# Dense experts of a PEER block: output blocks of three key rows instead of two, u split in halves

## The chip, the cores and the metric

The kernel runs on one core of a Trainium2 chip. The metric is the device time of one execution in microseconds (us), as the median of three runs. A profile of one further execution shows the engines: PE (TensorE, matmuls), PEld (its weight loads), DVE (VectorE), ACT (ScalarE), POOL (GpSimd) and SP, which issues DMA transfers.

## The reference, cut to what matters

One encoder layer over 1024 tokens of width 1024: a gated mixer of attention and convolution, then `h + PEER(RMSNorm(h))`, then a final RMSNorm. The change lies in PEER. It has 128 x 128 experts; each token picks 128 of them (8 heads, 16 each), with a gate each:

```
u = expert_u[eidx]
a = gelu(einsum('chkd,cd->chk', u, xc))
vv = expert_v[eidx]
return einsum('chk,chkd->cd', g * a, vv)
```

## The kernel before

The 8 token tiles of 128 are worked in two groups. The first five (`NB`) take the **dense** path: for each of the 128 key rows `i` (`NK`), all 128 experts of that row are computed for all 640 tokens, and the gate (`w_d`, zero where a token did not choose the expert) masks them. The last three (`NA`) take the **gather** path: for each token tile and each of its 128 choices, an indirect DMA on POOL brings one u row and one v row per token (`uvt`, L739, 128 x 2048 floats), DVE makes the dot product (L749), ACT the gelu and the gate (L751, L752), DVE adds the gated v row to `acc` (L754). That makes 3 x 128 = 384 such steps, called experts here, over four buffers of `uvt`. Both paths run side by side after the scores are done, from about 1316 us of the span to its end.

A key row `i` of the dense path is this chain. `expert_in(i)` loads u (`raw`, three buffers that u and v share), splits it into a high part (cast on ACT, L896) and a low part (subtract on DVE, L898), does 48 matmuls of 320 columns into `z` (L905; high x high, high x low, low x high), gelu on ACT (L929), multiplies by the gate tile `wt` on DVE (L930) and splits the product `p` in the same way. `expert_v(i)` loads and splits v. `expert_out` does p times v for ten output tiles of 128 x 512. Four of them (`held`) stay in PSUM until the end; six (`pout`, two PSUM buffers) are added to `hacc` in SBUF on DVE (L957) after each block of `BLK` key rows.

The order within an engine is set in three steps: the code's order; `tick`, which deals out the gather steps and the selection of experts by a running sum of matmul time (`GATHER`, 1.9 us a step); and a scheduler at build time, which may move an instruction past others of its engine and then fixes each engine's queue. On the chip each queue runs in that order. At the end `finish_rows` adds the held tiles, normalizes the five dense tiles and writes them out, while the rest of the gather steps runs.

Of the kernel before, what the change touches and what calls it, by code (L numbers as in the profile page):

```python
# [10 lines left out]
F32 = mybir.dt.float32  # L11
BF16 = mybir.dt.bfloat16
F32R = mybir.dt.float32r
I32 = mybir.dt.int32
U32 = mybir.dt.uint32
AF = mybir.ActivationFunctionType
# [4 lines left out]
P = 128  # L21
S = 1024
D = 1024
NT = S // P
KD = D // P
NB = 5
NA = NT - NB
GB = NB * P
# [7 lines left out]
NK = 128  # L36
# [6 lines left out]
NE = PH * TOPK  # L43

UVT = 4
PHB = 4
VHB = 3
BLK = 2
NR = 2
WB = 4  # L50
WT = 32
WQ = 4
WFB = 2
# [12 lines left out]
def block_kernel(ctx, tc, x, wqkv, wcols, wpr, wo, wq, skT, uv, uT, an_w, fn_w, fin_w, sub_w,  # L66
                 conv_w, lq1, lk1, lq2, lk2, cosT, sinT, out):
    nc = tc.nc
    V, A, PL, PE, SP = nc.vector, nc.scalar, nc.gpsimd, nc.tensor, nc.sync
# [4 lines left out]
    def pool(name, bufs=1, stack=None, **kw):  # L74
        return (stack or left).enter_context(tc.tile_pool(name=name, bufs=bufs, **kw))
# [19 lines left out]
    w_d = dram.tile([GB // WT, P, NK, WT], F32, name="w_d")  # L95
# [10 lines left out]
    def rows_bcast(pl, src, n, name, tag=None, bufs=None):  # L106
        t = pl.tile([P, n], F32, name=name, tag=tag or name, bufs=bufs)
        SP.dma_start(out=t, in_=bass.AP(tensor=src.tensor, offset=src.offset, ap=[[0, P], [1, n]]))
        return t
# [38 lines left out]
    def tick(us):  # L148
        for g in list(gens):
            g[1] -= us  # L150
            while g in gens and g[1] <= 0:
                g[1] += g[2]
                r = next(g[0], "end")
                if r == "end":
                    gens.remove(g)
                elif r:
                    g[2] = r
# [7 lines left out]
    def rstd_of(ss, n, width, tag):  # L165
        m = tiny.tile([P, width], F32, name=f"m_{tag}", tag=f"m_{tag}")
        V.tensor_scalar(m, ss, 1.0 / n, EPS, op0=ALU.mult, op1=ALU.add)
        r = tiny.tile([P, width], F32, name=f"r_{tag}", tag=f"r_{tag}")
        PL.tensor_tensor(r, m, mhalf[:, :width], op=ALU.pow)
        return r  # L170
# [9 lines left out]
    def operand(pl, shape, name, tag=None):  # L180
        return tuple(pl.tile(shape, F32R, name=name + c, tag=(tag or name) + c) for c in "hl")
# [276 lines left out]
    def halves(n):  # L458
        return [(0, n)] if n <= 512 else [(0, n // 2), (n // 2, n // 2)]
# [398 lines left out]
    n = NA * P  # L858
# [11 lines left out]
    hh, hl = operand(act, [P, KD, GB + 2], "actT")  # L870
# [17 lines left out]
    du, dn, dv, hp, gat = (pool(n) for n in ("du", "dn", "dv", "hp", "gat"))  # L888
# [1 line left out]
    hacc = hp.tile([P, NB - NR, D], F32, name="hacc")  # L890
    held = [[ps_r.tile([P, 512], F32, name=f"held{t}{hf}") for hf in range(2)] for t in range(NR)]

    def split(t, tag, bufs, shape, eng):
        pl = du if tag == "uh" else dv
        hi = pl.tile(shape, F32R, name=tag, tag=tag, bufs=bufs)
        A.copy(out=hi, in_=t)  # L896
        lo = pl.tile(shape, F32R, name=f"{tag}l", tag=f"{tag}l", bufs=bufs)
        eng.tensor_sub(lo, t, hi.bitcast(F32))  # L898
        return hi, lo

    def passes(ps, lhs, rhs, cols, first=True, last=True):
        n = len(lhs)
        for k in range(n):
            for j, (a, b) in enumerate(((0, 0), (0, 1), (1, 0))):
                PE.matmul(ps, lhsT=lhs[k][a], rhs=rhs[k][b],  # L905
                          start=first and k == 0 and j == 0, stop=last and k == n - 1 and j == 2)
        tick(cols / 2400 * 3 * n)

    wts = {}

    def raw_rows(src):
        t = du.tile([P, D], F32, name="raw", tag="raw", bufs=3)
        SP.dma_start(out=t, in_=src)
        return t

    def expert_in(i):
        b = i // WB
        if i % WB == 0:
            wts[b] = dn.tile([P, GB // WT, WB, WT], F32, name="wt", tag="wt", bufs=2)
            SP.dma_start(out=wts[b], in_=w_d[:, :, i:i + WB, :].rearrange("c p i t -> p c i t"))  # L920
        ur = raw_rows(uT[i])
        u = split(ur, "uh", 2, [P, D], V)
        us = [(u[0][:, k * P:(k + 1) * P], u[1][:, k * P:(k + 1) * P]) for k in range(KD)]
        hs = halves(GB)
        z = ps_z.tile([P, 2, 512], F32, name="z", tag="z")[:, :len(hs), :hs[0][1]]
        for j, (c0, cn) in enumerate(hs):
            passes(z[:, j, :], us, [(hh[:, k, c0:c0 + cn], hl[:, k, c0:c0 + cn]) for k in range(KD)], cn)
        p = dn.tile([P, GB], F32, name="pr", tag="pr", bufs=1)
        A.activation(p.rearrange("p (h c) -> p h c", h=len(hs)), z, AF.Gelu)  # L929
        V.tensor_mul(p.rearrange("p (c t) -> p c t", t=WT), p.rearrange("p (c t) -> p c t", t=WT),  # L930
                     wts[b][:, :, i % WB, :])
        return split(p, "ph", PHB, [P, GB], V)

    def expert_v(i):
        vr = raw_rows(uv[i * P:(i + 1) * P, D:])
        return split(vr, "vh", VHB, [P, D], V)

    resident = [(t, hf) for t in range(NR) for hf in range(2)]
    moving = [(t, hf) for t in range(NR, NB) for hf in range(2)]
    order = []  # L940
# [3 lines left out]
                order.append(q.pop(0))  # L944

    def expert_out(pv, vv, part, first, last):
        n = len(order) // BLK
        for t, hf in order[part * n:(part + 1) * n]:
            ds = slice(hf * 512, (hf + 1) * 512)
            lhs = [(p[0][:, t * P:(t + 1) * P], p[1][:, t * P:(t + 1) * P]) for p in pv]  # L950
            rhs = [(v[0][:, ds], v[1][:, ds]) for v in vv]
            if t < NR:
                passes(held[t][hf], lhs, rhs, 512, first, last)
            else:
                ps = ps_v.tile([P, 512], F32, name="pout", tag="v")
                passes(ps, lhs, rhs, 512)
                V.tensor_add(hacc[:, t - NR, ds], ps, hacc[:, t - NR, ds])  # L957

    def finish_rows():
        fin_b = rows_bcast(du, fin_w, D, "fin_d", "raw", 3)  # L960
        ss = tiny.tile([P, NB], F32, name="ss_f", tag="ss_f", bufs=1)
        ys = []
        for t in range(NB):
            if t < NR:
                y = raw_rows(h_d[t * P:(t + 1) * P, :])
                for hf in range(2):
                    ds = slice(hf * 512, (hf + 1) * 512)
                    V.tensor_add(y[:, ds], held[t][hf], y[:, ds])
            else:
                y = hacc[:, t - NR, :]  # L970
            A.activation(du.tile([P, D], F32R, name="uh", tag="uh", bufs=2), y, AF.Square, accum_out=ss[:, t:t + 1])
            ys.append(y)
        yield
        r = rstd_of(ss, D, NB, "f")
        yield
        for t in range(NB):
            V.scalar_tensor_tensor(ys[t], ys[t], r[:, t:t + 1], fin_b, op0=ALU.mult, op1=ALU.mult)
            SP.dma_start(out=out[t * P:(t + 1) * P, :], in_=ys[t])
            yield

    pv, vv = [], []
    for i in range(NK + BLK):
        if i < NK:
            pv.append(expert_in(i))
        b, part = i // BLK - 1, i % BLK
        if b >= 0:
            expert_out(pv[:BLK], vv[:BLK], part, b == 0, b == NK // BLK - 1)
            if part == BLK - 1:
                pv, vv = pv[BLK:], vv[BLK:]
        if i < NK:  # L990
            vv.append(expert_v(i))
        if i == 1:
            for t in range(NR, NB):
                SP.dma_start(out=hacc[:, t - NR, :], in_=h_d[t * P:(t + 1) * P, :])
    drain(sel)
    if gather in gens:
        gens.remove(gather)
    rows = finish_rows()
    for n in (6, 6, 1, 1, 1):
        next(rows)  # L1000
# [59 lines left out]
```

## Time and profile before

| what | value |
|---|---|
| median of 3 runs | 3186.92 us (3186.16 to 3197.02) |
| the profiled execution | 3202.99 us, span of its instructions 3201.2 us |
| PE busy | 3023.5 us (94%) |
| DVE busy | 2648.8 us (83%) |
| ACT, POOL busy | 1300.8 us (41%), 928.5 us (29%) |

The rows further down are from the trace of that profiled execution. Times are us from the start of its span. A row of the view by windows begins with the stretch and its length; then, where all engines are shown, follow the busy us and the number of instructions (x) of PE, PEld, DVE, ACT and POOL, then the mean granted PE clock (1.00 is full speed), the busy share of the 16 DMA engines and GB/s. A timeline row is start, duration, engine, line and operation; in square brackets stand the idle time ahead of it and what ended that.

### The profile page before, as it was taken

What the parts mean: (1) busy time and instruction counts of PE and PEld (TensorE: products, weight loads), DVE (VectorE), ACT (ScalarE), POOL (GpSimd) and SP (SyncE); (2) the same over time, 40 slices, a digit from 0 to 9 for tenths busy, and PEclk for the clock granted to TensorE, in tenths of its full rate; (3) what the DMA queues carried; (4) which work ended last, traced back from release to release, by engine and by line L of the source; (5) the groups of instructions that cost most, each with busy time, mean ns of one, the idle gap of its engine ahead of it and who ended that gap; (6) DMA issues with size and microseconds to landing.
All of it is one profiled execution on the core that took longest, in us unless ns stands there. A gap on an engine that the chain in (4) does not pass through costs nothing.

```text
span 3201.2 us, 45898 instructions
## 1 busy us (share of the span) xinstructions
PE 3023.5 (94%) x17551; PEld 2773.3 (87%) x17551; DVE 2648.8 (83%) x4661; ACT 1300.8 (41%) x2341; POOL 928.5 (29%) x712
## 2 busy tenths in 40 slices
PE   7999999898989989799999999999999999999994
PEld 6799998798988879789989989899898999999993
DVE  5442466379999996799999999999988999999998
ACT  3322364336567766433333333333333333333332
POOL 2310000036344444222332322222222323332333
PEclk9999999999999989899999999999999999999997
DMA  4451232555444375769888888798888999998987
GB/s 179 145 181 66 83 113 79 199 172 212 145 171 168 135 282 190 255 246 329 311 282 328 316 292 307 278 329 314 302 318 319 345 342 335 341 347 321 340 318 276
DMA packets 237549, 801.11 MB, mean 250 GB/s; under 512 B 18832, under 2 KB 123280, under 8 KB 174096
## 3 DMA queue, kind: packets, MB, share of 16 engines
q0 software_dynamic: 64704, 442.53, 37.3%
q1 hardware_dynamic: 152592, 305.30, 27.6%
q10 hardware_dynamic: 20032, 50.34, 4.1%
q8 instruction: 138, 2.26, 0.3%
q14 instruction: 83, 0.68, 0.1%
HBM read 714.74 MB, written 83.36 MB: 249 GB/s over the span
## 4 chain that ended last, share of the span: by engine, by line
PE 40%; issue 21%; DVE 16%; POOL 9%; DMA 9%; ACT 4%; SPq 0%; POOLq 0%; ACTq 0%; DVEq 0%
PE z L905 9%; POOL uvt L739 8%; PE pout L905 5%; PE pg L228 4%; PE held L905 4%; PE pq L228 3%; DMA uvt<-in_uv,idx 3%; PE ph L228 3%; DVE acc L754 2%; PE py L228 2%; DVE uvt L749 2%; PE pw L695 1%; PE ps L376 1%; PE pv L228 1%; DVE ms L714 1%
## 5 line engine op out<-in xcount | busy, mean ns | idle before, releaser
L739 POOL DMA_INDIRECT uvt<-in_uv,idx x384 | 533.2, 1389 | 1288.1 <-DVE acc L754 937.3
L905 PE MATMUL z<-actTh,uhl 128*128 128x320 f32 x2048 | 638.0, 312 | 4.0 <-DVE uhl L898 4.0
L905 PE MATMUL z<-actTh,uh 128*128 128x320 f32 x2048 | 637.4, 311 | 4.0 <-ACT pr L929 3.0
L905 PE MATMUL z<-actTl,uh 128*128 128x320 f32 x2048 | 637.0, 311 | 0.0
L749 DVE SCALAR_TENSOR_TENSOR uvt<-uvt,hng 128x1024 f32<-128x1024 f32 x384 | 471.4, 1230 | 54.3 <-DMA uvt<-in_uv,idx 53.6
L754 DVE SCALAR_TENSOR_TENSOR acc<-uvt,wt,acc 128x1024 f32<-128x1024 f32 x384 | 495.0, 1289 | 1.6 <-ACT wt L752 1.2
L905 PEld LDWEIGHTS z<-actTh,uh 128*128 128x128 f32 x2048 | 387.7, 189 | 15.7 <-ACT pr L929 3.7
L905 PEld LDWEIGHTS z<-actTh,uhl 128*128 128x128 f32 x2048 | 388.3, 190 | 11.6 <-DVE uhl L898 5.6
L905 PEld LDWEIGHTS z<-actTl,uh 128*128 128x128 f32 x2048 | 387.8, 189 | 9.9
L905 PE MATMUL pout<-vh,ph 128*128 128x512 f32 x768 | 304.0, 396 | 26.9 <-DVE hacc L957 14.0
L905 PE MATMUL pout<-vhl,ph 128*128 128x512 f32 x768 | 302.6, 394 | 0.6 <-DVE vhl L898 0.6
L905 PE MATMUL pout<-vh,phl 128*128 128x512 f32 x768 | 301.8, 393 | 0.0
L957 DVE TENSOR_TENSOR hacc<-pout,hacc 128x512 f32<-128x512 f32 x384 | 260.1, 682 | 21.2 <-PE pout L905 20.5
L718 POOL TENSOR_TENSOR o<-ms,wtr 128x512 f32<-128x512 bf16 x160 | 203.5, 1314 | 254.8 <-PE pw L695 134.8
L185 DVE TENSOR_TENSOR wl<-wr,wh 128x2048 fp32r<-128x2048 f32 x66 | 157.8, 2392 | 113.0 <-ACT wh L184 112.8
L751 ACT ACTIVATE wt<-zt 128x1 f32<-128x1 f32 x384 | 77.0, 201 | 417.0 <-DVE uvt L749 410.8
L896 ACT CAST uh<-raw 128x1024 fp32r<-128x1024 f32 x128 | 134.3, 1049 | 211.3 <-DMA raw<-in_uT 204.5
L184 ACT CAST wh<-wr 128x2048 fp32r<-128x2048 f32 x74 | 141.1, 1908 | 168.0 <-DMA wr<-in_wq 44.7
L695 PE MATMUL pw<-o,o 128*128 128x128 f32 x1280 | 172.3, 288 | 36.9 <-POOL o L718 19.4
L695 PEld LDWEIGHTS pw<-o,o 128*128 128x128 f32 x1280 | 164.4, 202 | 44.7 <-POOL o L718 25.3
L929 ACT ACTIVATE pr<-z 128x640 f32<-128x640 f32 x128 | 90.1, 704 | 275.4 <-PE z L905 254.6
L905 PE MATMUL held<-vhl,ph 128*128 128x512 f32 x512 | 200.3, 392 | 0.1
(290 smaller groups left out, 6758.6 us busy)
## 6 DMA issues: line engine op xcount, KB each, us to landing
raw<-in_uT SPq DMA_DIRECT2D x128, 512.0 KB
raw<-in_uv SPq DMA_DIRECT2D x128, 512.0 KB
w_d<-wbuf ACTq DMA_DIRECT2D x20, 2048.0 KB
wt<-w_d SPq DMA_DIRECT2D x32, 1280.0 KB
wr<-in_wcols SPq DMA_DIRECT2D x28, 1024.0 KB
wr<-in_wq SPq DMA_DIRECT2D x24, 1024.0 KB
xt<-in_x SPq DMA_DIRECT2D x16, 512.0 KB
q_d<-qt POOLq DMA_DIRECT2D x32, 256.0 KB
```

The lines of the kernel that those rows point to most:

```text
L184: A.copy(out=op[0][sl], in_=src)
L185: lo.tensor_sub(op[1][sl], src, op[0][sl].bitcast(F32))
L228: PE.matmul(pd, lhsT=l[a], rhs=r[b], start=i == 0 and j == 0, stop=i == n - 1 and j == len(c) - 1)
L695: PE.matmul(pw[:, u, :], lhsT=o2[:, t + u, :], rhs=o1[:, t + u, :], start=True, stop=True)
L718: PL.tensor_tensor(out=o1.rearrange("p t i -> p i t"), in0=ms[:, 0], in1=w[:, ts].unsqueeze(1).broadcast_to(sh), op=ALU.mult)
L739: PL.indirect_dma_start(out=t[:], out_offset=None, in_=uv, in_offset=bass.IndirectOffsetOnAxis(ap=sels[c][1][:, k:k + 1], axis=0))
L749: V.scalar_tensor_tensor(u, u, 1.0, st[c], op0=ALU.mult, op1=ALU.mult, accum_out=zt)
L754: V.scalar_tensor_tensor(st["acc"], v, wt, st["acc"], op0=ALU.mult, op1=ALU.add)
L896: A.copy(out=hi, in_=t)
L905: PE.matmul(ps, lhsT=lhs[k][a], rhs=rhs[k][b], start=first and k == 0 and j == 0, stop=last and k == n - 1 and j == 2)
L929: A.activation(p.rearrange("p (h c) -> p h c", h=len(hs)), z, AF.Gelu)
L957: V.tensor_add(hacc[:, t - NR, ds], ps, hacc[:, t - NR, ds])
```

## The change

Output blocks grow from two key rows to three (`BLK`), so `pout` and `held` gather nine matmuls instead of six before a tile is done, and 128 rows make 43 blocks, the last of two rows. u is cast and subtracted in two halves of 512 columns, each with its own buffers (three instead of two of the full width), and the matmuls of `z` take the first half for both column halves of `z`, then the second. The gate tile holds three key rows instead of four; p gets five buffers (was four), v gets four (was three).

```diff
-PHB = 4
-VHB = 3
-BLK = 2
+PHB = 5
+VHB = 4
+BLK = 3
-WB = 4
+WB = 3
...
     def expert_in(i):
-        b = i // WB
+        b, n = i // WB, min(WB, NK - i // WB * WB)
         if i % WB == 0:
             wts[b] = dn.tile([P, GB // WT, WB, WT], F32, name="wt", tag="wt", bufs=2)
-            SP.dma_start(out=wts[b], in_=w_d[:, :, i:i + WB, :].rearrange("c p i t -> p c i t"))
+            SP.dma_start(out=wts[b][:, :, :n, :], in_=w_d[:, :, i:i + n, :].rearrange("c p i t -> p c i t"))
         ur = raw_rows(uT[i])
-        u = split(ur, "uh", 2, [P, D], V)
-        us = [(u[0][:, k * P:(k + 1) * P], u[1][:, k * P:(k + 1) * P]) for k in range(KD)]
         hs = halves(GB)
         z = ps_z.tile([P, 2, 512], F32, name="z", tag="z")[:, :len(hs), :hs[0][1]]
-        for j, (c0, cn) in enumerate(hs):
-            passes(z[:, j, :], us, [(hh[:, k, c0:c0 + cn], hl[:, k, c0:c0 + cn]) for k in range(KD)], cn)
+        kh = KD // 2
+        for h in range(2):
+            u = split(ur[:, h * 512:(h + 1) * 512], "uh", 3, [P, 512], du)
+            us = [(u[0][:, k * P:(k + 1) * P], u[1][:, k * P:(k + 1) * P]) for k in range(kh)]
+            for j, (c0, cn) in enumerate(hs):
+                xs = [(hh[:, k, c0:c0 + cn], hl[:, k, c0:c0 + cn]) for k in range(h * kh, h * kh + kh)]
+                passes(z[:, j, :], us, xs, cn, h == 0, h == 1)
...
     def expert_out(pv, vv, part, first, last):
-        n = len(order) // BLK
-        for t, hf in order[part * n:(part + 1) * n]:
+        cut = [-(-len(order) * j // BLK) for j in range(BLK + 1)]
+        for t, hf in order[cut[part]:cut[part + 1]]:
...
-    for i in range(NK + BLK):
+    blocks = -(-NK // BLK)
+    for i in range((blocks + 1) * BLK):
...
-            expert_out(pv[:BLK], vv[:BLK], part, b == 0, b == NK // BLK - 1)
+            expert_out(pv[:BLK], vv[:BLK], part, b == 0, b == blocks - 1)
```

In the changed file the cast is L895, the subtract L897, the matmul L904, gelu L931, the gate L932 and the add to `hacc` L958.

On PE, in the middle of the dense path (near key row 90), the queue of before finishes a `pout` tile with two rows' p and v, three matmuls for each:

```order
L905 MATMUL pout_24515<-vh_24168,ph_24111 128x512
L905 MATMUL pout_24515<-vhl_24170,ph_24111 128x512
L905 MATMUL pout_24515<-vh_24168,phl_24113 128x512
L905 MATMUL pout_24515<-vh_24297,ph_24239 128x512
L905 MATMUL pout_24515<-vhl_24299,ph_24239 128x512
L905 MATMUL pout_24515<-vh_24297,phl_24241 128x512
```

The changed queue does so with three rows' (the same place):

```order
L904 MATMUL pout_24698<-vh_24057,ph_23995 128x512
L904 MATMUL pout_24698<-vhl_24059,ph_23995 128x512
L904 MATMUL pout_24698<-vh_24057,phl_23997 128x512
L904 MATMUL pout_24698<-vh_24184,ph_24138 128x512
L904 MATMUL pout_24698<-vhl_24186,ph_24138 128x512
L904 MATMUL pout_24698<-vh_24184,phl_24140 128x512
L904 MATMUL pout_24698<-vh_24318,ph_24265 128x512
L904 MATMUL pout_24698<-vhl_24320,ph_24265 128x512
L904 MATMUL pout_24698<-vh_24318,phl_24267 128x512
```

So the matmuls are as many as before (48 + 30 for each key row), and the tiles that DVE adds to `hacc` go from 3 to 2 for each key row, 384 to 258 in all.

On ACT, at the same place in the changed program, the casts of v for rows of the next block (`vh_24584` takes the buffer of `vh_24057`, which the matmuls just shown read last) stand ahead of the gather's gates and of the next gelu:

```order
L895 CAST ph_24666<-pr_24663 128x640
L895 CAST vh_24584<-raw_24582 128x1024
L895 CAST vh_24718<-raw_24716 128x1024
L751 ACTIVATE wt_22799<-zt_22797 128x1
L752 ACTIVATE wt_22799<-wt_22799,gw_12971 128x1
L895 CAST vh_24857<-raw_24855 128x1024
L751 ACTIVATE wt_22827<-zt_22825 128x1
L931 ACTIVATE pr_24792<-z_24726 128x640
```

Three casts of v stand together here, of which the first two wait for the last `pout` of the block before; in the queue of before it is two casts at a time.

On DVE, at the end of the program, the queue of before runs like this from its last adds to `hacc` on (L749 and L754 are the two halves of a gather step, L977 the final rows):

```order
L957 TENSOR_TENSOR hacc<-pout,hacc 128x512 x2
L754 SCALAR_TENSOR_TENSOR acc<-uvt,wt,acc 128x1024
L749 SCALAR_TENSOR_TENSOR uvt,zt<-uvt,hng 128x1024
L167 TENSOR_SCALAR m_f<-ss_f 128x5
L754 SCALAR_TENSOR_TENSOR acc<-uvt,wt,acc 128x1024
L749 SCALAR_TENSOR_TENSOR uvt,zt<-uvt,hng 128x1024
L754 SCALAR_TENSOR_TENSOR acc<-uvt,wt,acc 128x1024
L977 SCALAR_TENSOR_TENSOR raw<-raw,r_f,fin_d 128x1024 x2
L977 SCALAR_TENSOR_TENSOR hacc<-hacc,r_f,fin_d 128x1024 x3
L754 SCALAR_TENSOR_TENSOR acc<-uvt,wt,acc 128x1024
L749 SCALAR_TENSOR_TENSOR uvt,zt<-uvt,hng 128x1024 x3
L754 SCALAR_TENSOR_TENSOR acc<-uvt,wt,acc 128x1024 x3
```

The changed queue runs like this from its last add to `hacc` on:

```order
L958 TENSOR_TENSOR hacc<-pout,hacc 128x512
L749 SCALAR_TENSOR_TENSOR uvt,zt<-uvt,hng 128x1024
L754 SCALAR_TENSOR_TENSOR acc<-uvt,wt,acc 128x1024
L167 TENSOR_SCALAR m_f<-ss_f 128x5
L749 SCALAR_TENSOR_TENSOR uvt,zt<-uvt,hng 128x1024
L754 SCALAR_TENSOR_TENSOR acc<-uvt,wt,acc 128x1024
L749 SCALAR_TENSOR_TENSOR uvt,zt<-uvt,hng 128x1024
L978 SCALAR_TENSOR_TENSOR raw<-raw,r_f,fin_d 128x1024 x2
L978 SCALAR_TENSOR_TENSOR hacc<-hacc,r_f,fin_d 128x1024
L754 SCALAR_TENSOR_TENSOR acc<-uvt,wt,acc 128x1024
L978 SCALAR_TENSOR_TENSOR hacc<-hacc,r_f,fin_d 128x1024 x2
L749 SCALAR_TENSOR_TENSOR uvt,zt<-uvt,hng 128x1024 x2
```

Behind the rows shown, and up to the last L754, 23 L754 and 20 L749 stand in the changed queue. Behind its last add to `hacc` an L749 is followed at once by its own L754 in 13 places of the changed queue, and in 2 of that of before. The gather steps have moved back against the dense ones: ahead of the multiply by the gate of the 64th key row stand 170 of the 384 L754 in the queue of before and 168 in the changed one, ahead of the last such multiply 369 and 350; behind the last add to `hacc` stand 9 L754 and 7 L749 before, 26 and 25 in the changed queue.

## Rows read from the trace of the kernel before

**Rows 1.** View by windows, all engines, dense path and end.

```profile
1316.50:1348.90 32.40, 16.97 (x98) 16.36 (x99) 14.91 (x49) 8.88 (x9) 4.97 (x4) 0.81 1.02 373
1348.90:1787.60 438.70, 434.73 (x2400) 394.14 (x2400) 425.98 (x745) 147.28 (x299) 124.24 (x88) 0.99 0.84 299
...
2478.40:3133.50 655.10, 655.10 (x3666) 598.44 (x3666) 611.75 (x774) 228.13 (x484) 211.75 (x148) 1.00 0.92 336
3133.50:3159.90 26.40, 20.98 (x80) 14.86 (x78) 25.79 (x37) 10.36 (x25) 9.06 (x7) 0.94 0.83 301
3159.90:3201.20 41.30, 0.00 (x0) 0.00 (x0) 27.14 (x32) 5.78 (x18) 12.25 (x8) 0.53 0.68 247
```

**Rows 2.** View by windows, L930 alone (DVE, one for each key row).

```profile
1348.90:1787.60 438.70, 25.22 (x31) 0.99 0.84 299
1787.60:2244.30 456.70, 26.11 (x32) 1.00 0.85 306
2244.30:2478.40 234.10, 13.05 (x16) 0.99 0.86 312
2478.40:3133.50 655.10, 38.61 (x47) 1.00 0.92 336
```

**Rows 3.** Waits from 1360 to 2480 us: total, times, longest.

```profile
ACT vh L896 <- PE pout L905: 95.4, 30, 9.7
...
PE pout L905 <- DVE hacc L957: 11.4, 7, 4.8
```

**Rows 4.** Timeline of DVE from 3155 us to the end.

```profile
3158.71 1.28 DVE L957 TENSOR_TENSOR hacc<-pout,hacc 128x512 f32<-128x512 f32 x2
3159.91 1.27 DVE L754 SCALAR_TENSOR_TENSOR acc<-uvt,wt,acc 128x1024 f32<-128x1024 f32 x1
...
3166.89 2.48 DVE L977 SCALAR_TENSOR_TENSOR raw<-raw,r_f,fin_d 128x1024 f32<-128x1024 f32 x2
...
3172.87 1.28 DVE L754 SCALAR_TENSOR_TENSOR acc<-uvt,wt,acc 128x1024 f32<-128x1024 f32 x1
3174.07 1.22 DVE L749 SCALAR_TENSOR_TENSOR uvt<-uvt,hng 128x1024 f32<-128x1024 f32 x1
3175.21 0.08 DVE L749 DVE_READ_ACCUMULATOR uvt<-uvt,hng 128x1 f32 x1
...
3191.00 1.22 DVE L749 SCALAR_TENSOR_TENSOR uvt<-uvt,hng 128x1024 f32<-128x1024 f32 x1 [2.70 <-DMA uvt<-in_uv,idx]
...
3192.83 1.28 DVE L754 SCALAR_TENSOR_TENSOR acc<-uvt,wt,acc 128x1024 f32<-128x1024 f32 x1 [0.60 <-ACT wt L752]
...
3196.17 1.28 DVE L769 SCALAR_TENSOR_TENSOR acc<-acc,r_o,uvt 128x1024 f32<-128x1024 f32 x1 [0.68 <-POOL r_o L169]
```

**Rows 5.** View by windows, L754 alone (DVE, one for each expert).

```profile
2478.40:3133.50 655.10, 188.63 (x148) 1.00 0.92 336
...
3159.90:3201.20 41.30, 11.53 (x9) 0.53 0.68 247
```

**Rows 6.** Groups by line: subtract of u; busy, mean ns, idle before.

```profile
L898 DVE TENSOR_TENSOR uhl<-raw,uh 128x1024 fp32r<-128x1024 f32 x128 | 157.3, 1229 | 20.5 <-ACT uh L896 20.5
```

**Rows 7.** The chain that ended last, at the start of the dense path.

```profile
1326.33 20.00 DMA wt<-w_d
```

**Rows 8.** DMA view, 2400 to 3000 us: packets, MB, share of 16 engines; issues.

```profile
q0 software_dynamic: 19175, 139.66, 62.0%
q1 hardware_dynamic: 41152, 61.09, 29.7%
...
wt<-w_d SPq DMA_DIRECT2D x11, 1280.0 KB
```

**Rows 9.** Waits of DVE from 3159.9 us to the end.

```profile
DVE uvt L749 <- DMA uvt<-in_uv,idx: 7.0, 4, 2.7
```

**Rows 10.** Timeline of POOL near the end.

```profile
3182.76 1.95 POOL L739 DMA_INDIRECT uvt<-in_uv,idx  x1 [6.65 <-DVE acc L754]
```

More of the change, by code (lines that the diff above doesn't have):

```diff
@@ L891, in block_kernel, with split @@
     held = [[ps_r.tile([P, 512], F32, name=f"held{t}{hf}") for hf in range(2)] for t in range(NR)]
-    def split(t, tag, bufs, shape, eng):
-        pl = du if tag == "uh" else dv
+    def split(t, tag, bufs, shape, pl):
         hi = pl.tile(shape, F32R, name=tag, tag=tag, bufs=bufs)
@@ L897, in split @@
         lo = pl.tile(shape, F32R, name=f"{tag}l", tag=f"{tag}l", bufs=bufs)
-        eng.tensor_sub(lo, t, hi.bitcast(F32))
+        V.tensor_sub(lo, t, hi.bitcast(F32))
         return hi, lo
@@ L931, in expert_in @@
                      wts[b][:, :, i % WB, :])
-        return split(p, "ph", PHB, [P, GB], V)
+        return split(p, "ph", PHB, [P, GB], dv)
     def expert_v(i):
-        vr = raw_rows(uv[i * P:(i + 1) * P, D:])
-        return split(vr, "vh", VHB, [P, D], V)
+        return split(raw_rows(uv[i * P:(i + 1) * P, D:]), "vh", VHB, [P, D], dv)
     resident = [(t, hf) for t in range(NR) for hf in range(2)]
@@ L970, in finish_rows @@
                 y = hacc[:, t - NR, :]
-            A.activation(du.tile([P, D], F32R, name="uh", tag="uh", bufs=2), y, AF.Square, accum_out=ss[:, t:t + 1])
+            A.activation(dv.tile([P, D], F32R, name="vh", tag="vh", bufs=VHB), y, AF.Square, accum_out=ss[:, t:t + 1])
             ys.append(y)
```

## The prediction

> **What bounds the kernel now.** I read the view by windows first, over the stretch in which dense and gather path run side by side. From 2478.4 to 3133.5 us PE is busy in every microsecond of 655.1 [rows 1], and the gate multiply, one for each key row, comes 47 times in it [rows 2]: 655.1 / 47 = 13.94 us is what a key row costs PE with nothing in its way. That is the floor. The change keeps all 78 matmuls of a key row, so it keeps the floor.
>
> The other stretches are then held against it [rows 2]: 31 rows in 438.7 us are 6.6 us over it, 32 in 456.7 are 10.6 over, 16 in 234.1 are 11.1 over, 28 us in all. In these DVE is nearly full (425.98 of 438.7 us [rows 1]), and the waits name it: PE waited 11.4 us for adds to `hacc` [rows 3]. At the start of the dense path PE stands 15.4 of 32.4 us, and after the last gate multiply 5.4 of 26.4 [rows 1].
>
> Last, the end. After 3159.9 us PE does nothing for 41.3 us [rows 1]; DVE works there on the final rows [rows 4] and on the nine L754 that are left [rows 5], and the last of these ends the kernel. So there are two limits in a row: PE to about 3158 us, then whatever gather work DVE's queue still holds behind the dense work. The change acts on both.
>
> **The change part by part.** All durations on DVE below are spacings, from the start of one instruction to that of the next, since the rows' own durations overlap a little: an add to `hacc` 0.60 us (two in 1.20), L754 1.20, L749 1.14, the five final multiplies 5.98 together; an L749 followed at once by its own L754 costs 1.83 - 1.14 = 0.69 more, in which ACT makes the gate [rows 4].
>
> *Adds to `hacc`.* 126 of 384 go: 126 x 0.60 = 76 us, 0.59 us for each key row. *u in halves.* The subtract of 1024 columns takes 1.229 us [rows 6]; a half lies between half of it and the 0.68 us or so of an add of the same width, so two halves cost 0 to 0.13 us more. I take 0.1. ACT casts one piece more for each row and stands more than half of the time (147.28 busy of 438.7 us [rows 1]): nothing. So DVE gets back 0.5 us of each row. What that is worth is only the 28 us that PE loses in the middle, since after 2478 us PE loses nothing that could come back. Bounds 0 and 28; the first rows' DVE is also laden with the selection of experts, so I take 18. At the start PE waits for the first gate tile, which lands 20.0 us after its issue [rows 7]. It gets a quarter smaller, but the second one is now queued on SP right behind it. Between 5 us gained (a quarter of 20.0) and as much lost; I take 0.
>
> *Gate tiles of three rows.* A load still has 20 x 128 = 2560 runs, now of 384 bytes, and there are 43 loads instead of 32. Price of one load: the gathers' queue q0 moves 139.66 MB in 0.62 x 600 us, 375 KB/us; queue q1 used 0.297 x 600 = 178 us for 61.09 MB, of which 11 gate tiles are 14.4 MB [rows 8]. If the other 46.7 MB went at q0's rate (124 us), a gate tile took 54 / 11 = 4.9 us of all 16 engines. A changed load lies between 3.7 (by bytes) and 4.9 (by packets). At 4.9 the 43 take 54 us more than the 32, 0.4 us for each row. Against it stand fewer gathers in each row (next part): 148 L754 in 47 rows are 3.15 a row [rows 2, 5], the changed queue has 182 in the last 64 rows, 2.84; at 1.05 MB each that is 0.9 us less. The engines' share of 0.92 [rows 1] does not rise: nothing. But no row shows runs of 384 bytes, and a price of twice 4.9 us is not excluded: 43 x 9.8 - 32 x 4.9 = 265 us, 2.1 for each row, and the engines would be wanted for 0.92 x 13.94 + 2.1 - 0.9 = 14.0 us, just over PE's 13.94. (A rule speaks against this part too: the Trainium skill, "DMA: Bandwidth & Descriptors", section Specifications, asks for transfers of at least 512 bytes for full rate, and says that the engine reads, modifies and writes below that; by it the sum would be the one of the third rival below, by the rows it is the one I take.)
>
> *Five buffers of p and four of v, for blocks of three.* The cast of v that takes the buffer of the block before waits for the last `pout` of that block, and ACT's queue behind it holds gates of gathers and the next gelu. Such waits exist already (30 of them, 95.4 us, at most 9.7 [rows 3]), and PE loses little by them. In the changed queue that `pout` stands ahead of a whole run of 48 z matmuls (about 7 us), and two casts and two subtracts behind it need some 4.5 us before PE asks for them. I take 0; the price if the cover fails is among the rivals.
>
> *The place of the gathers.* This decides. DVE takes its queue in order, and the changed queue has 350 of 384 L754 ahead of the last gate multiply instead of 369. DVE has room for more there, but can't use it, because the steps stand further back. So first, from the last gate multiply to the last add to `hacc`: 8 L749, 8 L754, 10 adds, 4 adds of held tiles (0.60 each) and 2.6 us of splits and gate make 8 x 1.14 + 8 x 1.20 + 14 x 0.60 + 2.6 = 29.7 us, where before took 26.4 [rows 1]: +3. Then, behind the last add: 25 L749, 26 L754, the final multiplies and 13 places with the gate in the open: 28.5 + 31.2 + 6.0 + 9.0 = 74.7 us. The same sum for before (7, 9, 6.0, two places) gives 26.2; it took from 3159.9 to 3194.0, 34.1, and 7.0 of the difference are waits for gathers to land [rows 4, 9]. The changed tail thus takes between 74.7 (no wait) and 100 (one us for each gather, as now). A gather issued into an almost empty DMA took from 3182.76 to 3191.00 to be there [rows 4, 10], 8.2 us; with 3.0 for its L749 and L754 a buffer turns in 11.3 us, and four buffers give one each 2.8 us, under the 3.0 of the places with the gate in the open, a little over the 2.34 of the others. So few waits: 84. That is 50 more than before (41 to 66).
>
> **Sum.** -18 + 0 + 3 + 50 = +35 us on the profiled 3203 us, 1.1%. The profiled execution lies 0.5% over the median of the runs, so I carry the ratio over: 3187 x 3238 / 3203 = 3222 us. With all bounds for it -28 - 5 + 2 + 41 = +10 (3197), with all against it +5 + 5 + 66 = +76 (3263).
>
> **The rivals.** *PE gets all its idle time back.* If the room on DVE also cures the start and the last outputs, 28 + 15.4 + 5.4 = 49 us return, and against the 53 us of the longer tail that leaves +4: about 3191, not slower. For it: most of PE's named waits are on DVE. Against it: the start waits for a transfer, and the last outputs for DVE, which has more there than before. It decides from 37 us returned on (then less than 16 us, 0.5%, are left, about what a measurement of this kernel can tell from no change). Chance 0.14, of it 0.03 for a result faster than that.
>
> *The gathers don't go faster when they are alone.* Now one comes each 655.1 / 148 = 4.43 us [rows 5]. At that pace 25 take 111 us and the final multiplies 6: 33 more than I take, 3255. Against it: that pace is set by DVE's queue, busy 611.75 of 655.1 us [rows 1]. Chance 0.10.
>
> *The short runs fill the DMA engines*, as worked out above: u then lands late, and PE waits from the end of the selection on. For 64 rows at 0.1 to 0.5 us that is +6 to +32 on the forecast, about 3240. No row speaks for a doubled price but none excludes it. Chance 0.06.
>
> *The buffers are one short.* If of a wait of 9.7 us [rows 3] the 7 us of the z run cover only that much, 2.7 us in each of 43 blocks are 116 us: 3338, or half of it. Against it stands the order of the queues. Chance 0.05.
>
> **How the numbers follow.** My forecast, a longer tail with PE somewhat less hindered, has 0.65, with 3203 to 3245 as its own range; 0.05 of it may fall within 0.5%. Faster by over 0.5%: 0.03. Within 0.5%: 0.09 of the first rival and 0.05 of the forecast, 0.14. Slower by over 0.5%: the rest, 0.83. The range from 3194 to 3256 leaves out about half of the first two rivals and all of the last: 0.2 or a little less.
>
> **What would show it.** In the profile after: 2 adds to `hacc` for each row; in the middle, key rows at 13.9 to 14.0 us once the selection is over, with DVE at 80 to 88% instead of 93 and its waits on PE and on gathers larger; the last gate multiply some 18 us earlier (0 to 30); PE ending about 15 us earlier; and then about 90 us instead of 41 in which only DVE, POOL and ACT work, at 2.9 to 3.3 us for each gather. I am wrong if the tail is that long but PE ends 40 us or more earlier (first rival), if rows stay over 14.3 us with DVE waiting (buffers, or u landing late), or if the gathers of the tail come at over 4 us.

## The result and the profile after

The changed kernel is slower: 3233.82 us median (3230.21 to 3235.95, 4 runs) against 3190.36 us of before (3186.16 to 3197.02, 4 runs), a ratio of 1.0133 with a 95% interval of 1.0110 to 1.0156. Its profiled execution took 3230.21 us, with a span of 3228.4. In it the first gate multiply stands at 1341.0 us, the last at 3103.9, and the last add to `hacc` is over at 3133.7. The view by windows, cut there, answers to [rows 1]; columns as there.

```profile
1316.50:1341.00 24.50, 10.71 (x71) 10.19 (x69) 12.10 (x51) 6.37 (x8) 4.00 (x4) 0.82 1.03 396
1341.00:1787.60 446.60, 440.66 (x2452) 401.52 (x2453) 433.36 (x842) 158.94 (x339) 147.63 (x90) 0.99 0.84 300
...
2478.40:3103.90 625.50, 625.50 (x3506) 572.17 (x3505) 532.06 (x697) 212.16 (x479) 184.16 (x129) 1.00 0.87 314
3103.90:3133.70 29.80, 21.86 (x85) 16.01 (x83) 29.77 (x41) 10.62 (x28) 9.14 (x8) 0.94 0.77 270
3133.70:3228.40 94.70, 0.00 (x0) 0.00 (x0) 69.79 (x85) 14.74 (x54) 35.84 (x25) 0.50 0.83 303
```

DVE is relieved (532 of 625.5 us late in the dense path, 85%, where it was 93%), PE hardly stands any more, and then come 94.7 us without PE, where before had 41.3. The same view for the gate multiply alone (now L932), which answers to [rows 2]:

```profile
1787.60:2230.00 442.40, 27.82 (x32) 1.00 0.85 312
2230.00:2478.40 248.40, 14.77 (x18) 1.00 0.88 315
2478.40:3103.90 625.50, 36.11 (x44) 1.00 0.87 314
```

94 rows in 1316.3 us are 14.00 us a row; from the first gate multiply to the last, 127 rows in 1762.9 us, it is 13.88. So the floor of 13.94 is reached. The waits from 1360 to 2480 us, as [rows 3] (total, times, longest):

```profile
DVE hacc L958 <- PE pout L904: 25.6, 24, 2.0
ACT vh L895 <- PE pout L904: 20.4, 14, 3.0
...
PE pout L904 <- DVE hacc L958: 2.6, 2, 2.4
```

Now DVE waits for PE's outputs, and PE's wait for `hacc` fell from 11.4 us (7.3 in a second profile of before, e1 below) to 2.6. The timeline of DVE in the tail, as [rows 4]:

```profile
3133.05 0.68 DVE L958 TENSOR_TENSOR hacc<-pout,hacc 128x512 f32<-128x512 f32 x1
3133.82 1.23 DVE L749 SCALAR_TENSOR_TENSOR uvt<-uvt,hng 128x1024 f32<-128x1024 f32 x1
...
3163.91 1.22 DVE L749 SCALAR_TENSOR_TENSOR uvt<-uvt,hng 128x1024 f32<-128x1024 f32 x1
...
3165.74 1.28 DVE L754 SCALAR_TENSOR_TENSOR acc<-uvt,wt,acc 128x1024 f32<-128x1024 f32 x1 [0.60 <-ACT wt L752]
3166.94 1.22 DVE L749 SCALAR_TENSOR_TENSOR uvt<-uvt,hng 128x1024 f32<-128x1024 f32 x1
...
3207.43 1.22 DVE L749 SCALAR_TENSOR_TENSOR uvt<-uvt,hng 128x1024 f32<-128x1024 f32 x1 [2.44 <-DMA uvt<-in_uv,idx]
...
3220.27 1.28 DVE L754 SCALAR_TENSOR_TENSOR acc<-uvt,wt,acc 128x1024 f32<-128x1024 f32 x1 [0.60 <-ACT wt L752]
...
3223.61 1.28 DVE L769 SCALAR_TENSOR_TENSOR acc<-acc,r_o,uvt 128x1024 f32<-128x1024 f32 x1 [0.68 <-POOL r_o L169]
```

Besides the final rows, nothing but experts, one each 3.03 us where the gate lies in the open (3163.91 to 3166.94), now and then a short wait for a gather. L754 alone, over the dense rows and over the tail, as [rows 5]: 350 ahead, 26 behind.

```profile
1341.00:3103.90 1762.90, 450.31 (x350) 1.00 0.86 310
3133.70:3228.40 94.70, 33.34 (x26) 0.50 0.83 303
```

And the DMA view from 2400 to 3000 us, as [rows 8]:

```profile
q0 software_dynamic: 17323, 126.07, 56.9%
q1 hardware_dynamic: 49531, 61.60, 30.0%
...
wt<-w_d SPq DMA_DIRECT2D x15, 960.0 KB, 11.6
```

### The profile page after: what moved, and what is told of

The parts are those of the page before. It is cut to its first block, busy times and chain, and to the rows that moved or that the text cites. A ratio compares the mean times of both kernels' runs of the same rounds, so it can differ in the third digit from the quotient of the medians.

```text
span 3228.4 us, 46230 instructions
## 1 busy us (share of the span) xinstructions
PE 3008.1 (93%) x17551; PEld 2768.5 (86%) x17551; DVE 2585.4 (80%) x4663; ACT 1308.5 (41%) x2469; POOL 960.0 (30%) x712
## 4 chain that ended last, share of the span: by engine, by line
PE 62%; issue 13%; DVE 11%; POOL 6%; DMA 4%; ACT 4%; SPq 0%; POOLq 0%; ACTq 0%; DVEq 0%
PE z L904 20%; PE pout L904 11%; PE held L904 7%; PE pg L228 5%; POOL uvt L739 5%; PE pq L228 3%; PE ph L228 3%; PE pw L695 2%; PE py L228 2%; PE ps L376 1%; PE pv L228 1%; DMA wr<-in_wq 1%; PE pk L228 1%; PE po L228 1%; DVE ms L714 1%
## 5 line engine op out<-in xcount | busy, mean ns | idle before, releaser
L739 POOL DMA_INDIRECT uvt<-in_uv,idx x384 | 565.6, 1473 | 1299.4 <-DVE acc L754 1017.1
L904 PE MATMUL z<-actTh,uh 128*128 128x320 f32 x2048 | 635.9, 310 | 1.9 <-ACT wbuf L696 1.1
L904 PE MATMUL z<-actTh,uhl 128*128 128x320 f32 x2048 | 635.7, 310 | 0.7 <-DVE uhl L897 0.7
L904 PE MATMUL z<-actTl,uh 128*128 128x320 f32 x2048 | 635.9, 310 | 0.0
L754 DVE SCALAR_TENSOR_TENSOR acc<-uvt,wt,acc 128x1024 f32<-128x1024 f32 x384 | 493.9, 1286 | 19.4 <-ACT wt L752 18.5
L749 DVE SCALAR_TENSOR_TENSOR uvt<-uvt,hng 128x1024 f32<-128x1024 f32 x384 | 468.2, 1220 | 22.0 <-DMA uvt<-in_uv,idx 21.9
L904 PEld LDWEIGHTS z<-actTh,uh 128*128 128x128 f32 x2048 | 386.4, 189 | 8.7 <-ACT wbuf L696 1.3
L904 PEld LDWEIGHTS z<-actTl,uh 128*128 128x128 f32 x2048 | 386.0, 188 | 5.0
L904 PEld LDWEIGHTS z<-actTh,uhl 128*128 128x128 f32 x2048 | 387.5, 189 | 2.8 <-DVE uhl L897 1.6
L904 PE MATMUL pout<-vh,ph 128*128 128x512 f32 x768 | 302.6, 394 | 21.1 <-ACT ph L895 14.9
L904 PE MATMUL pout<-vhl,ph 128*128 128x512 f32 x768 | 301.5, 393 | 1.4 <-DVE vhl L897 1.4
L904 PE MATMUL pout<-vh,phl 128*128 128x512 f32 x768 | 300.1, 391 | 0.0
L895 ACT CAST uh<-raw 128x512 fp32r<-128x512 f32 x256 | 152.1, 616 | 181.3 <-PE z L904 141.6
L958 DVE TENSOR_TENSOR hacc<-pout,hacc 128x512 f32<-128x512 f32 x258 | 175.7, 684 | 60.6 <-PE pout L904 60.4
L931 ACT ACTIVATE pr<-z 128x640 f32<-128x640 f32 x128 | 90.4, 706 | 294.6 <-PE z L904 274.0
L904 PE MATMUL held<-vh,ph 128*128 128x512 f32 x512 | 199.7, 391 | 2.6 <-ACT ph L895 2.5
## 6 DMA issues: line engine op xcount, KB each, us to landing
wt<-w_d SPq DMA_DIRECT2D x42, 960.0 KB, 11.7
```

The costliest lines, as they stand in the source:

```text
L739: PL.indirect_dma_start(out=t[:], out_offset=None, in_=uv, in_offset=bass.IndirectOffsetOnAxis(ap=sels[c][1][:, k:k + 1], axis=0))
L749: V.scalar_tensor_tensor(u, u, 1.0, st[c], op0=ALU.mult, op1=ALU.mult, accum_out=zt)
L754: V.scalar_tensor_tensor(st["acc"], v, wt, st["acc"], op0=ALU.mult, op1=ALU.add)
L904: PE.matmul(ps, lhsT=lhs[k][a], rhs=rhs[k][b], start=first and k == 0 and j == 0, stop=last and k == n - 1 and j == 2)
```

## The experiments

A table first, since all kernels are read in the same way. "Dense" is the time from the first gate multiply to the last, "tail" the time from the end of the last add to `hacc` to the end of the span; beside each stands the number of L754 in it. Ratios are against before, run beside it on the same chip, with a 95% interval; before's own median went from 3190 to 3201 us from one such comparison to the next, so only ratios compare. Dense and tail are from one profiled execution of each kernel.

| kernel | ratio | dense, experts | tail, experts |
|---|---|---|---|
| e1_before | 1.0007 (0.9991 to 1.0023) | 1784.0, 369 | 41.2, 9 |
| changed kernel | 1.0133 (1.0110 to 1.0156) | 1762.9, 350 | 94.7, 26 |
| e2_wb3 | 1.0137 (1.0120 to 1.0154) | 1772.3, 348 | 102.6, 29 |
| e3_vh3 | 1.0118 (1.0098 to 1.0139) | 1825.6, 369 | 35.3, 8 |
| e4_blk3 | 1.0266 (1.0228 to 1.0303) | 1903.3, 384 | 13.0, 0 |
| e5_wb4_ph4 | 1.0011 (0.9987 to 1.0035) | 1839.9, 381 | 13.0, 0 |
| e6_ph4 | 1.0102 (1.0074 to 1.0131) | 1772.2, 354 | 83.9, 24 |
| e7_half | 1.0026 (1.0011 to 1.0041) | 1783.3, 367 | 48.1, 11 |
| e8_ph4_uh2_uvt5 | 0.9995 (0.9979 to 1.0011) | 1815.4, 374 | 24.9, 6 |
| e9_wb4_uh2 | 0.9920 (0.9893 to 0.9946) | 1784.0, 379 | 13.0, 0 |
| e10_wb4_lo | 1.0040 (1.0017 to 1.0063) | 1840.6, 384 | 13.0, 0 |
| e11_uh2 | 1.0123 (1.0095 to 1.0151) | 1765.3, 351 | 94.0, 26 |
| e12_blk2 | 1.0038 (1.0014 to 1.0063) | 1781.7, 362 | 59.5, 15 |

The last column is nearly one line: 13.0 + 3.1 x experts gives 40.9, 47.1, 59.5, 93.6 and 102.9 for 9, 11, 15, 26 and 29. e3 and e6 lie 2.5 and 3.5 us under it (37.8 and 87.4), and only e8, the one with a fifth buffer for gathers, well under it (31.6). The expectations count the tail from the start of that last add, hence their 13.7.

**Before again (e1_before).** No edit.

> The kernel before, unchanged. The profiled execution of before (3203.0 us) lies above all its timed runs, while that of the changed kernel lies at the low end of its own. If that execution was only a slow one, the time here is that of before (ratio 1.000, bounds 0.996 to 1.004), and a second profile has a span some 10 to 14 us below 3201; the stretch that gets shorter is then the one to compare the changed kernel with. If profiling itself costs before 12 us, the second span is again near 3200.

```profile
1335.20:3119.20 1784.00, 1766.56 (x9814) 1604.68 (x9815) 1690.17 (x2532) 612.09 (x1261) 540.12 (x381) 1.00 0.88 317
3144.90:3186.10 41.20, 0.00 (x0) 0.00 (x0) 27.00 (x31) 5.75 (x18) 12.13 (x7) 0.50 0.67 247
```

The windows of its dense part and tail. Its span is 3186.1 us, 15.1 less than in the first profile, though the program is the same: 11.2 of them lie ahead of the first gate multiply (1335.2, not 1346.4), 3.9 in the dense part (1784.0, not 1787.9), and none in the tail. The ten runs of e1 went from 3186.92 to 3205.58 us (median 3196.55), so the first profile (3202.99) is of one of the longer executions and this one (3187.92) of one of the shortest, and differences of some 10 us at the start between two profiles are no effect of a change. Against this profile the changed kernel has +5.8 ahead of the first gate multiply, -21.1 in the dense part, +4.1 to the last add to `hacc` (29.8, not 25.7) and +53.5 in the tail: +42.3, which agrees with the medians (+43.5); the changed kernel's profile too is of its shortest execution.

**Gate tiles of three rows alone (e2_wb3).**

```diff
-WB = 4
+WB = 3
...
-        b = i // WB
+        b, n = i // WB, min(WB, NK - i // WB * WB)
...
-            SP.dma_start(out=wts[b], in_=w_d[:, :, i:i + WB, :].rearrange("c p i t -> p c i t"))
+            SP.dma_start(out=wts[b][:, :, :n, :], in_=w_d[:, :, i:i + n, :].rearrange("c p i t -> p c i t"))
```

> Before with gate tiles of three rows and nothing else. In its queue 29 experts stand behind the last add to hacc instead of 9. Theory 1 (the place of the gathers decides): from the two tails an expert there costs (87.8 - 34.1) / 17 = 3.2 us, so the tail is 34 + 20 x 3.2 = 97 us, 63 more; the dense rows get back 0 to 28 us, since 21 experts fewer stand ahead of their end. Together +35 to +63 on 3190: 3225 to 3253. Theory 2 (what costs is the load in runs of 384 bytes): the dense rows get longer, PE stands more in the middle than the 28 us of before, and the time lies over 3253. Theory 3 (the gate tile is harmless, it is the larger blocks and buffers that move the gathers on the chip): within 10 us of before.

```profile
1339.40:3111.70 1772.30, 1761.89 (x9829) 1605.09 (x9828) 1636.56 (x2433) 600.07 (x1219) 511.38 (x360) 1.00 0.86 309
3138.60:3241.20 102.60, 0.00 (x0) 0.00 (x0) 76.83 (x93) 16.22 (x60) 40.46 (x28) 0.50 0.84 312
```

Theory 1 holds, in time (3240.72 us) and in place (a tail of 102.6 us with 29 experts). This one constant costs as much as the whole change. It does so with PE freer in the dense part (1772.3 - 1761.9 = 10.4 us idle, 17.4 in e1): no slowing of the rows by the short runs shows. What the edit does is in the queue: the scheduler at build time puts 29 experts behind the dense work instead of 9.

**Three buffers of v (e3_vh3) and blocks of three alone (e4_blk3).** Both bring the experts forward and keep v at three buffers.

e3, on the changed kernel:

```diff
-VHB = 4
+VHB = 3
```

e4, on before, with the cut of `order` and the count of blocks as in the changed kernel:

```diff
-BLK = 2
+BLK = 3
```

> The changed kernel with three buffers of v instead of four, all else as changed, the short runs too. In its queue 8 experts stand behind the last add to hacc instead of 26. Theory 1 (the place of the gathers): the dense part keeps what it gained, 30 us to the last gate multiply, and the tail falls back to about 31 us: 3190 - 30 + 3 - 3 = 3160 us, 3150 to 3175 with what more gathers ahead take back. Theory 2 (the short runs): 3220 or more, since they are all still there. Theory 3 (the buffers of v carry the gain): a cast of v that waits for the last pout of the block holds PE up by up to 2.7 us in each of 43 blocks, so 3160 plus up to 116, and PE's idle time in the middle shows it.

> Before with output blocks of three rows alone: u whole, gate tile of four rows, four buffers of p and three of v as before. In its queue all 384 experts stand ahead of the last add to hacc. Theory 1 (the place of the gathers): the tail is the final rows alone, some 10 us instead of 34; DVE has 0.59 us less of each row in adds to hacc and 0.28 more in experts, so PE gets back between 0 and 28 us of the middle: 3190 - 24 - 0 to 28 = 3138 to 3166. Theory 3 (three buffers of v are too few for blocks of three): PE stands up to 2.7 us in each of 43 blocks, 3160 to 3280, with the waits of v's cast for pout as the row that shows it.

Theory 1 alone failed here. The tails are about as short as it said (35.3 and 13.0 us), but the dense part grew by 62.7 and, against e1, by 119.3 us. Theory 2's bound for e3 is met as well (3235.98 us), but the short runs are no part of e4, which grew more. The dense windows of e3 and of e4:

```profile
1344.10:3169.70 1825.60, 1776.87 (x9797) 1605.42 (x9798) 1617.74 (x2490) 618.68 (x1385) 573.27 (x381) 0.99 0.85 310
1345.30:3248.60 1903.30, 1804.48 (x9796) 1622.83 (x9797) 1655.04 (x2448) 612.49 (x1290) 580.47 (x393) 0.97 0.85 304
```

A wait of PE in e3 from 1345 to 3100 us:

```profile
PE pout L904 <- DVE vhl L897: 18.6, 15, 2.8
```

The changed kernel has no such wait in that stretch, and e9 below, with 379 experts ahead and four buffers of v, has 0.8 us of it: with four buffers v is ready when the block's outputs start, with three it isn't. The fourth rival's mechanism is real, and VHB = 4 is what kept it away. In e3, 62.7 / 43 = 1.46 us for each block are lost, a part of them to the 19 more experts ahead (below: some 13 us). Of the 62.7, 40.9 are idle time of PE (48.7, not 7.9), in which the wait shown is the largest, and 21.8 its busy time (1776.87, not 1755.04 us), at a mean granted clock of 0.99 instead of 1.00. In e4 that clock is 0.97: in or right behind each of PE's five longest waits there (4.4 to 7.0 us, the first gate multiplies aside) it fell to the lower of its two levels, 1.2 GHz, for 6.8 to 10.2 us.

For e4 theory 3 is not shown. Its 3284.88 us lie just over the range, and the row that was to show it did not come: from 1400 to 3100 us ACT's casts of v waited 9.8 us for `pout`, 135.4 in e1. PE waited, from 1345 us on, for adds to `hacc` (28.2 us), v (23.1 in three rows), gelu (22.6) and u (15.4 in two); e4 has four buffers of p besides three of v, and which of them is short stays open.

**The gate tile of four rows, paid for with a buffer of p (e5_wb4_ph4), and that buffer by itself (e6_ph4).**

On the changed kernel; e6 has the first pair alone.

```diff
-PHB = 5
+PHB = 4
...
-WB = 3
+WB = 4
```

> The changed kernel with the gate tile of four rows again, paid for with one buffer of p less (four instead of five); four buffers of v, blocks of three and halves of u stay. Its queue has 381 of 384 experts ahead of the last gate multiply and none behind the last add to hacc (changed kernel: 350 and 26). Theory 1 (the place of the gathers alone, as long as PE finds its operands): the dense part keeps the 30 us, the tail of 34 falls to 10: 3195 - 30 - 24 = 3141 us, 3130 to 3165. Theory 3 (blocks of three need more buffers; three of v cost 62 us from the first gate multiply to the last add to hacc): with four buffers of p the second p of a block is already held up by the last pout of the block before; 0.5 to 1.5 us in each of 43 blocks are 20 to 65 us more: 3160 to 3205. Theory 4 (four buffers of uvt can't bring an expert each 4.7 us): DVE waits for gathers far more than the 11 us of the changed kernel and the dense rows get longer by that.

> The changed kernel with four buffers of p instead of five, nothing else: the price of that buffer by itself. In its queue 24 experts stand behind the last add to hacc (26). Theory 1: 2 experts fewer in the tail are 6 us less, 3227 us, 3220 to 3235. Theory 3: as for the run before, 20 to 65 us more than that, 3245 to 3290, with a wait of p's cast for pout or of PE for p in each block.

The fifth buffer of p is worth 9 us while 24 experts stand behind (1772.2, not 1762.9), less than theory 3 said; in e6 theory 1 holds (3232.59 us, ratio 1.0102 for 1.0133). Theory 3's wait is there, p's cast for `pout` (108.0 us, 38 times, from 1400 to 3100 us; 7.6 in the changed kernel), but PE lost little by it. With the experts forward the same four buffers go with a dense part of 1839.9 us, 77 more, and with 3201.18 us in all: theory 1 missed, theory 3's range holds it. That profile is of the longest of e5's ten executions (3224.55 us), so 77 is too much for a usual one. Theory 4 finds a little: DVE waited 50.3 us for gathers from 1400 to 3100 us, against 10.8 in the changed kernel and 43.2 in e1. It doesn't explain 77.

**u in halves alone (e7_half)** is the changed file with `PHB`, `VHB`, `BLK` and `WB` as before. **A fifth uvt buffer (e8_ph4_uh2_uvt5)** is the changed kernel with `UVT` 5, `PHB` 4 and two buffers for the halves.

> Before with u split in halves of a row and nothing else (blocks of two rows, gate tile of four, four buffers of p and three of v). 11 experts stand behind the last add to hacc instead of 9. DVE and ACT have one more instruction for each row, 0.1 us on DVE, which is hidden in the middle or takes at most 13 us; the tail gets 2 x 3.2 = 6 us longer; the first gelu may come some 5 us earlier, since the first half of u is split in half the time. Theory 1: 3190 to 3210. If the halves are what made the dense part of the changed kernel faster, the last gate multiply comes 25 us earlier instead and the time is about 3175.

> The changed kernel with a fifth buffer of uvt, paid for with one buffer of p (four) and one of the halves of u (two); gate tile of three rows, short runs and all, four buffers of v. Its queue has 374 experts ahead of the last gate multiply and 6 behind the last add to hacc. Theory 1: tail of about 25 us, so 3195 - 30 - 9 = 3156 us, 3145 to 3175. Theory 2 (the short runs cost time on the DMA engines once the gathers come faster): 3185 and more, with u landing late. Theory 3: 20 to 65 us over the first, whatever the run with four buffers of p alone shows.

Halves alone do nothing for the dense part (1783.3, not 1784.0) and lengthen the tail by two experts, as theory 1 said. In e8 again the experts came forward and the dense part grew (1815.4), and the two cancel: ratio 0.9995 and 3200.93 us, where theory 1 had 3145 to 3175. Theory 2's sign is absent, since ACT waited 2.8 us for u to land from 1400 to 3100 us (35.8 in the changed kernel); theory 3's range holds it.

**All buffers and the gate tile of four rows (e9_wb4_uh2, e10_wb4_lo), with two halves as control (e11_uh2).** What e3 to e8 leave open is whether an expert ahead is costly in itself or only where a buffer is missing.

e9, on the changed kernel (`ident_r` and the scratch tile `jk` move in the same way; `pcon` is given back before the dense path). e11 has the last pair alone.

```diff
-    ident = const.tile([P, P], F32, name="ident")
+    ident = pcon.tile([P, P], F32, name="ident")
...
-WB = 3
+WB = 4
-            u = split(ur[:, h * 512:(h + 1) * 512], "uh", 3, [P, 512], du)
+            u = split(ur[:, h * 512:(h + 1) * 512], "uh", 2, [P, 512], du)
```

e10, as e9 but with a number of buffers of its own for the low part (the last argument of `split`):

```diff
-            u = split(ur[:, h * 512:(h + 1) * 512], "uh", 2, [P, 512], du)
+            u = split(ur[:, h * 512:(h + 1) * 512], "uh", 3, [P, 512], du, 2)
...
-        return split(p, "ph", PHB, [P, GB], dv)
+        return split(p, "ph", PHB, [P, GB], dv, 4)
```

> The changed kernel with the gate tile of four rows again, and with all five buffers of p and four of v. The room comes from two buffers instead of three for the halves of u, and from three small tiles (the identity in two types and a scratch tile) that now lie in a pool which is given back before the dense path. Its queue has 379 of 384 experts ahead of the last gate multiply and none behind the last add to hacc. In nine kernels so far the end lies 13.7 + 3.1 x (experts behind) us after the last add to hacc; that gives 14 us here. Theory 3 (missing buffers of p and v made the dense part of the earlier runs longer): the gate multiplies run from first to last in 1763 to 1780 us as in the changed kernel, and the time is 1342 + 1770 + 26 + 14 = 3152 us, 3145 to 3170, faster than both. Theory 5 (an expert that stands ahead is paid for in the dense rows, at about its 2.3 to 2.5 us of DVE, however many buffers there are): 26 x 2.5 = 65 us more, 1828 us from first to last and 3210 in all, 3195 to 3220. Theory 6 (two halves of u are too few): as theory 5 in time, but then the run with two halves alone shows it too, by 10 us or more.

> As the run before, but with three buffers for the high part of the halves of u and two for the low part, and five for the high part of p and four for the low part. All 384 experts stand ahead of the last gate multiply. Theory 3: 1763 to 1780 us from first to last gate multiply, 9 us more if four low parts of p cost what four p cost (1772.2 against 1762.9 us); 3145 to 3175 in all. Theory 5: 34 x 2.5 = 85 us more, 1848 and 3230 in all, 3205 to 3240.

> The changed kernel with two buffers instead of three for the halves of u and nothing else; 26 experts stand behind the last add to hacc, as in the changed kernel. If two halves are enough: the time of the changed kernel, 3234 us within 6. Theory 6: 10 to 45 us more, with PE waiting for uh and uhl (in the run with the fifth uvt buffer, four p and two halves it waited 15 us for them).

e9 is faster than both kernels, 0.992. Its windows:

```profile
1347.60:3131.60 1784.00, 1762.61 (x9804) 1604.10 (x9805) 1648.19 (x2556) 624.16 (x1406) 567.49 (x391) 1.00 0.89 323
...
3156.60:3169.60 13.00, 0.00 (x0) 0.00 (x0) 6.25 (x7) 1.15 (x2) 1.18 (x1) 0.64 0.50 202
```

The dense windows of e11 and of e10:

```profile
1346.60:3111.90 1765.30, 1753.91 (x9797) 1601.17 (x9798) 1585.93 (x2464) 609.54 (x1350) 557.99 (x363) 1.00 0.86 310
1347.20:3187.80 1840.60, 1779.55 (x9795) 1611.04 (x9796) 1660.10 (x2569) 636.49 (x1416) 558.71 (x393) 0.99 0.87 315
```

e9 and e11 differ in the gate tile (and where three small tiles lie): 28 more experts ahead make the dense part 1784.0 - 1765.3 = 18.7 us longer, 0.67 us for each, where behind they cost 3.1. (The gate tile changes along with the experts in this pair, as it does from e1 to e2; nothing here has the price of an expert ahead by itself.) So theory 5 is wrong with its 2.3 to 2.5 us, and theory 3 nearly right, and too hopeful by 4 us at the upper end of its dense part. Theory 6 falls with e11 (1765.3 against 1762.9). e10 lands in theory 5's range (3213.31 us), though e9 with nearly the same order of experts does not. What e10 lacks beside e9 is one buffer for the low part of p, and its dense part is 1840.6 us. Its PE waits there:

```profile
PE z L904 <- ACT pr L931: 22.1, 18, 7.0
...
PE pout L904 <- DVE hacc L958: 17.9, 13, 3.3
```

In e9 these are 6.1 and 0.8. By these profiles the fifth buffer of p (of its low part at least) is worth 53 us with the experts forward: 56.6, less some 3 for five experts more ahead (384, not 379); from e5 it is 77 less 31 x 0.67 for its experts, 56. But both are of the longest execution of their kernel (e10's took 3224.78 us, the median of its seven 3213.31), while e9's is its median. By the ratios, each good to some 8 us, e5 lies 29 us over e9 and e10 38. So some 30 to 40 us is the safer price, still more than the 9 of e6. By what chain that buffer leads to these two waits the runs don't take apart.

**Blocks of two rows in e9 (e12_blk2).**

```diff
-BLK = 3
+BLK = 2
```

> The fastest kernel so far (gate tile of four rows, two buffers for the halves of u, five of p, four of v) with blocks of two rows instead of three, nothing else: what the blocks of three bring by themselves. Its queue has 15 experts behind the last add to hacc (0 with blocks of three) and 362 ahead of the last gate multiply (379). If the blocks of three are what makes room on DVE: a tail of 13.7 + 15 x 3.1 = 60 us, 1775 to 1790 us from first to last gate multiply, 3205 to 3225 in all, over before by 0.2 to 0.8%. If it is the buffers and not the blocks: 3171 us within 10, and the adds to hacc that come back find room on DVE.

```profile
1343.50:3125.20 1781.70, 1765.75 (x9815) 1605.81 (x9816) 1683.68 (x2632) 623.45 (x1374) 506.44 (x373) 1.00 0.87 313
3153.10:3212.60 59.50, 0.00 (x0) 0.00 (x0) 42.80 (x51) 9.27 (x32) 18.89 (x14) 0.51 0.78 286
```

As the first theory said, within a microsecond in its tail. With the same buffers blocks of three make 1.0038 into 0.992: not by a faster dense part (1784.0 and 1781.7), but because DVE takes 17 experts more into the same time.

## Why the prediction was right, point by point

*What bounds the kernel.* Two limits in a row, PE and then DVE's queue behind it: so it is in every run, though with no expert behind only the final rows are left for the second (13.0 us). The floor of 13.94 us a row was reached.

*Adds to `hacc`, u in halves: -18.* It measured -21.1 against e1 (-25.0 against the first profile), within 0 to -28. But the reason was only half of it, so that the number came out is in part luck. I gave it to the 0.5 us that the adds free. e2 frees no adds and gains 11.7 us with 21 experts fewer in the rows (0.56 us each). By 0.56 to 0.67 the 19 experts that left here are 11 to 13 us, and the blocks, halves and buffers together the other 8 to 10. Halves alone: 0.7 us. Nor was it idle time of PE alone: that fell by 9.5 us (17.4 in e1, 7.9 here), and the busy time by 11.5 (1766.56 and 1755.04 us), which no term has and no run explains. The bound of 28 was too wide, too:

```profile
1346.40:3134.30 1787.90, 1769.05 (x9813) 1607.56 (x9814) 1689.79 (x2531) 611.79 (x1261) 534.92 (x381) 0.99 0.88 316
```

In the first profile of before the 127 rows from the first gate multiply to the last take 17.5 us more than 127 x 13.94, with PE idle for 18.9; the 28 came from three stretches cut at whole rows.

*The start: 0.* It read -5.4 or +5.8, by which profile of before one takes; e1 shows that this is the spread of executions.

*Gate tiles of three rows: nothing.* On the DMA engines that was right. By the working of the prediction, q1 used 180 us, and the 46.9 MB that are no gate tile took 127 of them at q0's 369 KB/us, so a tile took 53 / 15 = 3.5 us; in e2 it comes to 4.6. The bounds were 3.7 and 4.9; neither is near 9.8, and the third rival falls. The traces' records of single packets say it without that working: from 2400 to 3000 us the 28160 packets of 512 bytes in before took 29.7 ns each in the mean, the 36211 of 384 bytes in the changed kernel 22.9, and 2560 of them take 4.8 and 3.7 us of the 16 engines. So the price goes nearly by bytes. (The Trainium skill, "DMA: Bandwidth & Descriptors", section Specifications, asks for at least 512 bytes a transfer for full rate and has the engine read, modify and write below that; here the measurement differs: runs of 384 bytes, loaded from HBM into SBUF, move 16.8 bytes in a ns and those of 512 17.2.) But the step is the weakest of the prediction all the same: as a part of the change this is the one that costs, through the place of the gathers, which I read from the queue and tied to no part.

*Five buffers of p and four of v: 0.* Right, and now with a price: one v less is some 50 us by e3's profile (62.7, less 13 for the experts) and some 40 by its ratio, one p less 9 us or, with the experts forward, some 30 to 40.

*The last gate multiply to the last add: +3.* 29.8 us for 29.7 worked out; against before +4.1.

*The tail: +50 (41 to 66).* +53.5. From the last add to the end of the last L754 it was 87.8 us for the 84 taken, and the 11 us or so of waits for gathers are a little more than I gave. One reading in it was wrong: the DMA engines were not almost empty while that gather of before was under way (share 0.80 from 3182 to 3191 us), and in the changed tail they are nearly full (0.97 from 3140 to 3180). That the gathers kept up as estimated holds; whether four buffers or full engines set what waits there are stays open (for the buffers speaks e8, whose tail with five lies 6.7 us under the line of the table).

*The sum.* +35 for +42.3; 3.5 of the difference are the tail, 5.8 the start of that execution, 1 the last rows, and the dense part goes 3 the other way. First and second rival fall: the dense part got 21 to 25 us shorter, not 40, and the gathers came at 3.0 us in the tail, not 4.43. One sign was wrong: DVE waited less for gathers, not more (10.8 us from 1400 to 3100, 43.2 in e1).

## What to carry to other kernels

Where one queue serves two paths, count what it still holds when the other path ends, and price it: here 3.1 us for each expert behind, 0.6 for each ahead where no buffer is missing. A part that touches neither path's arithmetic can move that count through the scheduler, as the gate tile did, so build each part of a change alone and look at the queue. Filling the freed engine needs the buffers as well: with the experts forward the ratio was 0.992 with all of them, 1.0011 and 1.0040 with a buffer of p or of its low part missing, and 1.0118 with one of v missing.

## What the runs showed that was not expected

The same program, profiled twice, differed by 15.1 us of 3200, three quarters of it ahead of the stage under study; before's timed runs went from 3184.57 to 3212.26 us in all. And in the tail, with PE silent and little but gathers to load, the DMA engines' share was still 0.83, and DVE waited up to 2.44 us for a gather. Why the scheduler puts experts later for gate tiles of three rows stays open; the runs show only that it does, and what that costs.
